# Block forms with their signs turned: one GpSimd sum becomes an accumulating DMA, the other moves to VectorE

## The chip, the cores and the metric

The kernel runs on one core of a Trainium2 chip. The metric is the device time of one execution in microseconds (us); the times of several executions are given as their median with the lowest and the highest. Five engines with queues of their own do the work: TensorE (PE in the profile, its weight loads PEld), VectorE (DVE), ScalarE (ACT), GpSimd (POOL) and SyncE (SP, which here only issues DMAs). An engine carries out its instructions in the order in which they stand in its queue, and an instruction that has to wait holds everything behind it.

## The reference

One layer of an encoder over 512 tokens of width 1024, in float32. What matters here are the projections: products of a weight matrix with the normed activations.

```python
def hybrid_mixer(h, w_in, ...):
    p = h @ w_in
    q, k, v, z, cb, cc, cx, gates = jnp.split(p, SPLIT_IDX, axis=-1)
    ...                                     # three branches ya, yb, yc of width 512
    br_d = jnp.einsum("bsnc,ncd->bsnd", br, w_branch)
    g = jax.nn.sigmoid(gates.reshape(bsz, seq, N_BRANCHES, D_MODEL))
    return jnp.sum(g * br_d, axis=2) @ w_out

def memory_cross_attention(h, mem, mem_g, wq, wk, wv, wo):
    m = rms_norm(mem, mem_g)
    q = (h @ wq).reshape(bsz, seq, XA_HEADS, XA_HEAD_DIM)
    ...

def swiglu(h, w_gate, w_up, w_down):
    return (jax.nn.silu(h @ w_gate) * (h @ w_up)) @ w_down
```

The layer is x + mixer(norm x), then + attention into 256 memory tokens, then + swiglu, and a last norm.

## The kernel before

**Two halves for each factor.** A float32 factor goes to TensorE as a rounded part "hi" (float32r, made by a cast on ScalarE) and the remainder "lo" = value - hi (a subtraction on VectorE). A product is three passes: hi x hi, hi x lo, lo x hi. In tile names a last h or l tells the two (wh, wl; hTh, hTl; h3h, h3l). A weight block arrives in a raw tile wr (three buffers), loaded by SyncE as soon as a buffer is free.

**Seven products for eight.** The gates of the mixer (class Branch, 11 steps of 256 columns), the queries of the cross-attention (Query, 4 steps) and the gate and up projections of the feed-forward (Gate and Up in turn, 20 steps) use the class Seven. It cuts the weight block and the activations in 2 x 2 blocks (rows 0-511 and 512-1023 of the inner dimension; 128 columns; 256 tokens) and makes the 2 x 2 block product from 7 block products, with sums and differences of blocks, the forms: s1 to s4 on the weight side, t1 to t4 on the activation side. Inside the raw tile `r[:, 0:4, 0:P]` and `r[:, 0:4, P:256]` are the two upper blocks, `r[:, 4:8, ...]` the lower ones. The form s1 has a tile s of its own; s3 is put in place of the upper right block, s2 in place of the upper left one and s4 in place of the lower left one.

**Steps.** `seven_open` prepares the first item, and `seven_run` goes through the items with one step each. In step k TensorE multiplies item k (n in the code) and finishes two products of the one before (p), while the other engines make the forms, casts and remainders of the one after (q). A step has these products in this order on TensorE: l11 with r11 and s1 with t1 of item n, s4 with r22 of item p, s2 with t2 of n, l22 with t4 of p, l12 with r21 of n (into a bank pfb), s3 with t3 of n; 12 matmuls of 256 columns each. Branch steps end with 24 matmuls of 512 columns (pbr), from a fourth kind of weight tile, wb.

**Who makes what before the change.** For item q: GpSimd makes s1 (L251) and then s3 (L252); VectorE makes s2 from them (L257) and s4 (L258); ScalarE casts the left blocks, s1 and the pair (s2, s4) in one instruction (L268), and VectorE takes the remainders (L273). The blocks s3 and l22 are the right half of the raw tile; they are cast only in the next step, at its beginning, in one instruction of 1024 elements a partition (`n.hi(("s3", "l22"), n.right)`). Only for the first item of the feed-forward stage does VectorE make s1 and s3 too. In the results, ScalarE copies a product out of PSUM (L287, tiles m and u) and VectorE adds the next one to it (L886, L1362 and others, called c11, c22, c12 in the code).

**What sets the order.** All of this in Seven is pinned: it stands on its engine in the order of the code. The rest is ordered by a list scheduler when the program is built.

## Time and profile before

| | us |
|---|---|
| median of 3 runs (lowest to highest) | 945.65 (945.56 to 946.8) |
| the profiled execution | 946.39 |
| its span, first to last instruction | 944.4 |
| PE busy / PEld busy in it | 933.3 / 846.9 |
| DVE busy | 717.8 |
| ACT busy | 500.3 |
| POOL busy | 241.0 |

Busy time counts an engine's instructions; what the engine waited for stands in the view of waits. The profiled execution is 0.74 us above the median and within the range of the runs; 1.99 us of it lie outside its span. A row of the timeline has the start, the duration (of the first to the last, where several are merged), engine, line, operation, tiles with sizes, how many, and in brackets the idle time before it and what ended it. The stages that use Seven are Branch (about 241 to 404 us), Query (501 to 545) and Gate/Up (637 to 831).

### The profile page before, as it was taken

How to read it: one execution, taken by the hardware profiler on the slowest of the kernel's cores; microseconds unless marked ns; L12 is line 12 of the kernel's file. 1: busy time of each engine (PE TensorE's matmuls, PEld its weight loads, DVE VectorE, ACT ScalarE, POOL GpSimd, SP SyncE). 2: the span in 40 equal slices, each digit the busy share in tenths (PEclk: the TensorE clock that was granted, in tenths of full speed). 3: DMA queues.
4: the chain of work that ended last, by engine and by line, in shares of the span. 5: the costliest groups of instructions: out<-in, count | busy, mean ns of one | idle time of the engine just before them, and what ended most of it. 6: DMA issues, size and time to landing. Idle time of an engine off the chain costs nothing.

```text
span 944.4 us, 14872 instructions
## 1 busy us (share of the span) xinstructions
PE 933.3 (99%) x6054; PEld 846.9 (90%) x6054; DVE 717.8 (76%) x891; ACT 500.3 (53%) x780; POOL 241.0 (26%) x216
## 2 busy tenths in 40 slices
PE   8999999999999999999999999999999999999997
PEld 8988888888999999988989998899999999988885
DVE  6787887658866666576897783498888888777996
ACT  6574665334544344356754762555555545557452
POOL 0221122254311535230013000024535454201000
PEclk9999999999999999999999999999999999999999
DMA  8421221320333323272352421114233332376622
GB/s 290 157 90 51 84 79 56 123 90 23 112 107 117 110 92 112 90 266 91 142 171 90 133 91 45 45 46 134 91 115 110 101 123 92 110 268 150 243 99 89
DMA packets 84276, 109.24 MB, mean 116 GB/s; under 512 B 2176, under 2 KB 63664, under 8 KB 84208
## 3 DMA queue, kind: packets, MB, share of 16 engines
q1 hardware_dynamic: 82384, 101.74, 32.5%
q0 software_dynamic: 1824, 6.55, 2.6%
q8 instruction: 47, 0.77, 0.3%
q14 instruction: 21, 0.17, 0.1%
HBM read 104.10 MB, written 2.10 MB: 112 GB/s over the span
## 4 chain that ended last, share of the span: by engine, by line
PE 94%; DVE 2%; ACT 1%; DMA 1%; issue 1%; SPq 0%; POOL 0%; POOLq 0%; DVEq 0%; ACTq 0%
PE pf L281 29%; PE pb L143 9%; PE pn L143 7%; PE pbr L929 7%; PE pc L143 6%; PE pfb L281 5%; PE pq L143 4%; PE pb L1432 4%; PE pf L143 4%; PE pa L1432 3%; PE pc L1432 3%; PE pk L143 2%; PE pv L494 2%; PE z L694 2%; PE po L143 1%; PE sc L143 1%
## 5 line engine op out<-in xcount | busy, mean ns | idle before, releaser
L273 DVE TENSOR_TENSOR wl<-wr,wh 128x1024 fp32r<-128x1024 f32 x105 | 152.8, 1465 | 33.6 <-ACT wh L268 33.6
L268 ACT CAST wh<-wr 128x1024 fp32r<-128x1024 f32 x105 | 110.3, 1053 | 31.7 <-DVE wr L258 31.7
L106 DVE TENSOR_TENSOR wl<-wr,wh 128x1024 fp32r<-128x1024 f32 x68 | 83.6, 1244 | 33.0 <-ACT wh L105 23.4
L105 ACT CAST wh<-wr 128x1024 fp32r<-128x1024 f32 x68 | 70.2, 1051 | 41.8 <-PE pb L143 19.3
L251 POOL TENSOR_TENSOR s<-wr 128x512 f32<-128x512 f32 x34 | 45.2, 1328 | 166.3 <-DVE w L273 126.7
L287 ACT COPY u<-pf 128x256 f32<-128x256 f32 x70 | 26.2, 374 | 100.3 <-DVE g L1362 31.5
L252 POOL TENSOR_TENSOR wr<-wr 128x512 f32<-128x512 f32 x34 | 71.1, 2091 | 2.7
L177 POOL TENSOR_TENSOR rs<-ve,mhalf 128x1 f32<-128x1 f32 x18 | 10.8, 602 | 228.4 <-DVE ve L175 228.4
L937 POOL TENSOR_TENSOR merged<-merged,sg 128x512 f32<-128x512 f32 x16 | 26.8, 1679 | 80.7 <-DVE sg L936 80.7
L711 POOL TENSOR_SCALAR_AFFINE_SELECT ab<-ab 128x128 f32<-128x128 f32 x32 | 23.6, 770 | 79.8 <-ACT ab L708 79.8
L287 ACT COPY m<-pf 128x256 f32<-128x256 f32 x35 | 13.0, 373 | 46.5 <-PE pf L281 45.7
L281 PE MATMUL pf<-h3th,wh 128*128 128x256 f32 x240 | 37.0, 276 | 0.0
L281 PE MATMUL pf<-h3tl,wh 128*128 128x256 f32 x240 | 37.0, 276 | 0.0
L281 PE MATMUL pf<-h3th,wl 128*128 128x256 f32 x240 | 37.0, 276 | 0.0
L258 DVE TENSOR_TENSOR wr<-wr 128x512 f32<-128x512 f32 x35 | 33.0, 943 | 1.2
L1468 ACT CAST wh<-wr 128x1024 fp32r<-128x1024 f32 x20 | 20.8, 1053 | 21.2 <-PE pc L1432 9.6
L281 PEld LDWEIGHTS pf<-h3th,wh 128*128 128x128 f32 x240 | 31.7, 188 | 0.1
L281 PEld LDWEIGHTS pf<-h3th,wl 128*128 128x128 f32 x240 | 31.7, 188 | 0.0
L281 PEld LDWEIGHTS pf<-h3tl,wh 128*128 128x128 f32 x240 | 31.7, 188 | 0.0
L186 ACT ACTIVATE jk<-xr 128x512 f32<-128x512 f32 x24 | 15.1, 630 | 24.4 <-DVE xr L1019 13.5
L257 DVE TENSOR_TENSOR wr<-s,wr 128x512 f32<-128x512 f32 x35 | 23.9, 684 | 4.7 <-POOL wr L252 4.3
L1389 POOL TENSOR_TENSOR afb<-afb,g 128x256 f32<-128x256 f32 (+1 forms) x16 | 18.4, 1153 | 34.7 <-DVE afb L1362 34.7
(433 smaller groups left out, 2717.0 us busy)
## 6 DMA issues: line engine op xcount, KB each, us to landing
wr<-in_w_in_dram SPq DMA_DIRECT2D x26, 1024.0 KB, 5.4
wr<-in_w_down_ffn_dram SPq DMA_DIRECT2D x13, 1024.0 KB, 5.8
wr<-in_w_gate_ffn_dram SPq DMA_DIRECT2D x11, 1024.0 KB, 5.6
wr<-in_w_up_ffn_dram SPq DMA_DIRECT2D x11, 1024.0 KB, 5.3
wb<-in_w_branch_dram SPq DMA_DIRECT2D x12, 512.0 KB, 3.4
wr<-in_w_out_dram SPq DMA_DIRECT2D x4, 1024.0 KB, 8.5
wr<-in_w_k_xa_dram SPq DMA_DIRECT2D x4, 1024.0 KB, 8.3
wr<-in_w_v_xa_dram SPq DMA_DIRECT2D x4, 1024.0 KB, 5.0
```

What stands on the lines that cost most here:

```text
L105: nc.scalar.copy(out=hi, in_=src)
L106: nc.vector.tensor_tensor(out=lo, in0=src, in1=hi, op=ALU.subtract)
L143: mm = nc.tensor.matmul(dst, a(i), b(j), start=first and n == 0, stop=last and n == tot - 1)
L251: pin(self.eng.tensor_tensor(out=self.s1, in0=r[:, 0:4, P:256], in1=r[:, 4:8, P:256], op=ALU.add))
L252: pin(self.eng.tensor_tensor(out=r[:, 0:4, P:256], in0=r[:, 0:4, 0:P], in1=r[:, 0:4, P:256], op=ALU.subtract))
L258: pin(nc.vector.tensor_tensor(out=r[:, 4:8, 0:P], in0=r[:, 4:8, 0:P], in1=r[:, 0:4, 0:P], op=ALU.subtract))
L268: pin(nc.scalar.copy(out=t[0], in_=src))
L273: pin(nc.vector.tensor_tensor(out=l, in0=src, in1=h, op=ALU.subtract))
L281: pin(nc.tensor.matmul(dst[:, 0:256], w[:, k, :], v[:, k, :], start=first and n == 0, stop=last and n == 11, skip_group_check=True))
L287: pin(nc.scalar.copy(out=m, in_=self.a[:, 0:256]))
L929: pin(nc.tensor.matmul(pbr, self.wb[w][:, i, j * P:(j + 1) * P], y[v][:, i, :], start=m == 0, stop=m == 3 * CT - 1))
L1432: pin(nc.tensor.matmul(dst, a[u][:, k, :], w[v][:, k, :], start=first and n == 0, stop=last and n == 5, skip_group_check=True))
```

## The change

The forms on the activation side that were subtracted one way round are subtracted the other way, so that on the weight side every form is a sum. With R11, R12, R21, R22 for the raw weight blocks: s1 = R12 + R22 as before, s3 = R12 + R11 (was R11 - R12), s2 = s1 + R11 (was s1 - s3), s4 = R21 + s2 (was R21 - s2). s3 is now added up in place by two accumulating DMAs of 256 KB each on GpSimd's queue; s1 is made on VectorE; s2 is written into the tile of s1 and no longer needs s3. So (s2, s4) no longer lie side by side, and their cast and their remainder become two instructions of 512 elements each. Some products come out with the other sign, which is put right where they are used: by `scale=-1.0` of an activation, or by the new helper `minus` (-a - b in one VectorE instruction) or another scalar_tensor_tensor in place of a tensor_tensor.

```diff
+    def minus(o, a, b):
+        return nc.vector.scalar_tensor_tensor(out=o, in0=a, scalar=-1.0, in1=b, op0=ALU.mult, op1=ALU.subtract)
...
     class Seven:
-        eng = nc.gpsimd
...
         def sums(self):
             r = self.raw
             self.s1 = self.fp.tile([P, 4, P], F32, name=nm("s1"), tag="s1", bufs=1)
-            pin(self.eng.tensor_tensor(out=self.s1, in0=r[:, 0:4, P:256], in1=r[:, 4:8, P:256], op=ALU.add))
-            pin(self.eng.tensor_tensor(out=r[:, 0:4, P:256], in0=r[:, 0:4, 0:P], in1=r[:, 0:4, P:256], op=ALU.subtract))
+            pin(nc.vector.tensor_tensor(out=self.s1, in0=r[:, 0:4, P:256], in1=r[:, 4:8, P:256], op=ALU.add))
+            for k in (0, 2):
+                pin(nc.gpsimd.dma_start(out=r[:, k:k + 2, P:256], in_=r[:, k:k + 2, 0:P], accum_op=ALU.add))
 
         def sums2(self):
             r = self.raw
-            pin(nc.vector.tensor_tensor(out=r[:, 0:4, 0:P], in0=self.s1, in1=r[:, 0:4, 0:P], op=ALU.subtract))
-            pin(nc.vector.tensor_tensor(out=r[:, 4:8, 0:P], in0=r[:, 4:8, 0:P], in1=r[:, 0:4, 0:P], op=ALU.subtract))
+            pin(nc.vector.tensor_tensor(out=self.s1, in0=self.s1, in1=r[:, 0:4, 0:P], op=ALU.add))
+            pin(nc.vector.tensor_tensor(out=r[:, 4:8, 0:P], in0=r[:, 4:8, 0:P], in1=self.s1, op=ALU.add))
...
-            pin(nc.scalar.copy(out=t[0], in_=src))
-            return t, src
+            n = t[0].shape[1] // len(src)
+            got = [(t[0][:, i * n:(i + 1) * n], t[1][:, i * n:(i + 1) * n], v) for i, v in enumerate(src)]
+            for h, l, v in got:
+                pin(nc.scalar.copy(out=h, in_=v))
+            return got
...
     # prepare and seven_run
             if q:
-                q.sums2()
+                q.lo(c)
...
             if q:
-                q.lo(c)
+                q.sums2()
...
-                b = q.hi(("s2", "s4"), q.left)
+                b = q.hi(("s2", "s4"), q.s1, q.left[:, 4:8])
...
     # right_forms, query_forms and forms_right, the activation side, three places like this one
-        for o, a, b in ((r11, r12, r11), (r12, r22, r12), (r22, r22, r11), (r21, r21, r22)):
+        for o, a, b in ((r11, r11, r12), (r12, r22, r12)):
             nc.vector.tensor_tensor(out=o, in0=a, in1=b, op=ALU.subtract)
+        minus(r22, r22, r11)
+        minus(r21, r22, r21)
...
     # where the results are used
         def gate22(self):
-            self.silu(self.g[:, 1, HT[1]], self.g[:, 1, HT[1]])
+            self.silu(self.g[:, 1, HT[1]], self.g[:, 1, HT[1]], -1.0)
...
     class Up(Gate):
         def c22(self, p, m):
-            self.add(self.af[:, 1, HT[1]], p, m)
+            pin(minus(self.af[:, 1, HT[1]], p, m))
...
         def c21(self, p):
-            self.mul_g(nc.vector, 1, HT[0], p)
+            pin(nc.vector.scalar_tensor_tensor(out=self.af[:, 1, HT[0]], in0=p, scalar=-1.0,
+                                               in1=self.gate.g[:, 1, HT[0]], op0=ALU.mult, op1=ALU.mult))
...
-    items[0].eng = nc.vector
```

On GpSimd the sums go and two DMA issues stand in their place. The rows are those of two steps of the Gate/Up stage, an Up item's products af in the middle; wr is a raw weight tile, s the tile of s1. Before:

```order
L251 TENSOR_TENSOR s_7218<-wr_7079 128x512
L252 TENSOR_TENSOR wr_7079<-wr_7079 128x4x128
L251 TENSOR_TENSOR s_7340<-wr_7202 128x512
L252 TENSOR_TENSOR wr_7202<-wr_7202 128x4x128
L1389 TENSOR_TENSOR afb<-afb,g_7185 128x256
L1389 TENSOR_TENSOR afb<-afb,g_7185 128x512
L251 TENSOR_TENSOR s_7463<-wr_7324 128x512
L252 TENSOR_TENSOR wr_7324<-wr_7324 128x4x128
```

And after the change:

```order
L254 DMA wr_7145<-wr_7145 128x2x128 x2
L254 DMA wr_7271<-wr_7271 128x2x128 x2
L1402 TENSOR_TENSOR afb<-afb,g_7254 128x256
L1402 TENSOR_TENSOR afb<-afb,g_7254 128x512
L254 DMA wr_7396<-wr_7396 128x2x128 x2
L254 DMA wr_7522<-wr_7522 128x2x128 x2
```

The two DMAs of an item stand where its two sums stood, ahead of the products of the same step.

On VectorE one step of the same stage, from the sum c11 of one item to that of the next; wl and w are remainders, g the tile of the sums. Before:

```order
L1362 TENSOR_TENSOR g_7185<-pfb_7171,m_7101 128x256
L1362 TENSOR_TENSOR g_7185<-pf_7082,u_7199 128x256
L273 TENSOR_TENSOR wl_7222<-wr_6957,wh_7221 128x1024
L273 TENSOR_TENSOR wl_7253<-wr_7079,wh_7252 128x1024
L1362 TENSOR_TENSOR g_7185<-pf_7082,u_7151 128x256
L257 TENSOR_TENSOR wr_7079<-s_7218,wr_7079 128x4x128
L258 TENSOR_TENSOR wr_7079<-wr_7079 128x4x128
L273 TENSOR_TENSOR w_7257<-s_7218,w_7256 128x512
L273 TENSOR_TENSOR wl_7291<-wr_7079,wh_7290 128x1024
```

After:

```order
L1375 TENSOR_TENSOR g_7254<-pfb_7239,m_7168 128x256
L1375 TENSOR_TENSOR g_7254<-pf_7148,u_7268 128x256
L252 TENSOR_TENSOR s_7287<-wr_7145 128x512
L278 TENSOR_TENSOR wl_7292<-wr_7020,wh_7291 128x1024
L278 TENSOR_TENSOR wl_7323<-wr_7145,wh_7322 128x1024
L1375 TENSOR_TENSOR g_7254<-pf_7148,u_7217 128x256
L278 TENSOR_TENSOR w_7327<-s_7287,w_7326 128x512
L259 TENSOR_TENSOR s_7287<-s_7287,wr_7145 128x512
L260 TENSOR_TENSOR wr_7145<-wr_7145,s_7287 128x4x128
L278 TENSOR_TENSOR wl_7361<-s_7287,wh_7360 128x512
L278 TENSOR_TENSOR wl_7361<-wr_7145,wh_7360 128x512
```

The sum s1 (L252) has come in behind the two sums of the results, the remainder of s1 now stands ahead of the sums s2 and s4, and the last remainder is in two halves.

On ScalarE the entry of the Branch stage: the casts of the first item (left blocks; s1; s2 and s4; then s3 with l22, wr again), and the first copy out of PSUM, m. Before:

```order
L268 CAST wh_2151<-wr_2144 128x1024
L268 CAST w_2157<-s_2146 128x512
L268 CAST wh_2161<-wr_2144 128x1024
L268 CAST wh_2212<-wr_2144 128x1024
L287 COPY m_2215<-pf_2195 128x256
```

After:

```order
L273 CAST wh_2152<-wr_2144 128x1024
L273 CAST w_2156<-s_2146 128x512
L273 CAST wh_2162<-s_2146 128x512
L273 CAST wh_2162<-wr_2144 128x512
L273 CAST wh_2216<-wr_2144 128x1024
L292 COPY m_2219<-pf_2198 128x256
```

Only the cast of (s2, s4) is cut in two; the cast of s3 with l22, the second from below, is where it was, and now it reads what the two DMAs have written.

TensorE's 6,054 matmuls stand in the same order in both programs, with the same operands at the same addresses in SBUF and PSUM, and so do SyncE's DMAs.

## The prediction

> **What bounds the kernel now.** I read the page's busy times first, then what TensorE waited for, then the chain that ended last, and last the busy time in the three stages that the change touches.

> ```profile
> span 944.4 us, 14872 instructions
> ...
> PE 933.3 (99%) x6054; PEld 846.9 (90%) x6054; DVE 717.8 (76%) x891; ACT 500.3 (53%) x780; POOL 241.0 (26%) x216
> ```

> TensorE is busy for 933.3 of 944.4 us. So at most 11.1 us could be won without taking matmuls away, and the change takes none away. Where the idle time lies is the next question: the view of waits, TensorE alone, all of its rows.

> ```profile
> PE warm L527 <- POOL ident masks.py:199: 1.4, 1, 1.4
> PE pc L143 <- DVE kk L657: 0.9, 1, 0.9
> PE pv L494 <- ACT hTh L469: 0.8, 1, 0.8
> PE pv L494 <- ACT wvh L478: 0.7, 1, 0.7
> ```

> Four waits with a releaser, 3.8 us in all, at lines of the first norm and of the attention branch (tiles warm, pv, kk); no line of Seven is among them. A busy TensorE is not yet one at its best pace, since the ends of matmuls are modelled. The chain that ended last has the pace in its rows: of a Branch step (the first) and of a Gate/Up step (the two others).

> ```profile
> 246.85 8.34 PE pf L281 x72
> ...
> 642.14 8.16 PE pf L281 x72
> 650.30 1.36 PE pfb L281 x12
> ```

> A Gate/Up step is 84 matmuls in 9.52 us, 113.3 ns each, and the chain goes through TensorE alone. The stages by windows (Branch, Query, Gate/Up):

> ```profile
> 245.43:400.63 155.20, 155.20 (x1106) 145.47 (x1106) 102.45 (x126) 67.99 (x114) 51.15 (x31) 1.00 0.34 109
> 501.67:542.00 40.33, 40.25 (x347) 40.06 (x346) 33.69 (x54) 26.50 (x50) 7.02 (x4) 1.00 0.37 122
> 636.68:824.40 187.72, 187.72 (x1646) 186.87 (x1646) 158.13 (x187) 100.18 (x168) 84.38 (x55) 1.00 0.35 110
> ```

> The columns are the length, then busy time of PE, PEld, DVE, ACT and POOL with instructions, granted clock, DMA share, GB/s. In all three the matmul unit is idle for 0.08 us together, at a granted clock of 1.00. This is the ceiling of what a quicker VectorE or GpSimd can win there. The order of the matmuls and their addresses stay, so only two things can move the time: a wait that the new order brings, or another pace.

> **The sums leave GpSimd.** These are the two sums of a step on GpSimd, and VectorE's remainders:

> ```profile
> L273 DVE TENSOR_TENSOR wl<-wr,wh 128x1024 fp32r<-128x1024 f32 x105 | 152.8, 1465 | 33.6 <-ACT wh L268 33.6
> ...
> L251 POOL TENSOR_TENSOR s<-wr 128x512 f32<-128x512 f32 x34 | 45.2, 1328 | 166.3 <-DVE w L273 126.7
> ...
> L252 POOL TENSOR_TENSOR wr<-wr 128x512 f32<-128x512 f32 x34 | 71.1, 2091 | 2.7
> ```

> 116.3 us of GpSimd go, off the path. What they did to others stands in a Gate/Up step of the timeline, all engines:

> ```profile
> 680.32 1.29 POOL L251 TENSOR_TENSOR s<-wr 128x512 f32<-128x512 f32 x1 [1.23 <-DVE w L273]
> ...
> 680.76 1.93 DVE L273 TENSOR_TENSOR wl<-wr,wh 128x1024 fp32r<-128x1024 f32 x1 [0.19 <-ACT wh L268]
> ...
> 681.69 2.15 POOL L252 TENSOR_TENSOR wr<-wr 128x512 f32<-128x512 f32 x1
> ...
> 683.14 0.37 ACT L287 COPY u<-pf 128x256 f32<-128x256 f32 x1 [2.41 <-DVE g L1362]
> ...
> 683.54 0.43 DVE L1362 TENSOR_TENSOR g<-pf,u 128x256 f32<-128x256 f32 x1 [0.52 <-ACT u L287]
> ...
> 684.14 0.62 PE L281 MATMUL pf<-h3h,wh 128*128 128x256 f32 x4
> ...
> 684.49 1.22 DVE L273 TENSOR_TENSOR wl<-wr,wh 128x1024 fp32r<-128x1024 f32 x1 [0.53 <-ACT wh L268]
> ...
> 685.75 0.37 SPq L114 DMA_DIRECT2D wr<-in_w_gate_ffn_dram  x1
> ...
> 685.88 0.63 ACT L268 CAST w<-s 128x512 fp32r<-128x512 f32 x1
> ...
> 687.68 0.37 ACT L287 COPY u<-pf 128x256 f32<-128x256 f32 x1 [1.17 <-DVE g L1362]
> ...
> 692.68 1.05 ACT L268 CAST wh<-wr 128x1024 fp32r<-128x1024 f32 x1
> ```

> The same remainder takes 1.93 us beside GpSimd's sums and 1.22 us without, 0.71 more. That one counts: behind it on VectorE stands c11, then ScalarE copies u, then VectorE's c22 (683.54 to 683.97) reads the bank to which TensorE adds from 684.14 on. The margin is 0.17 us. It grows to about 0.9 us, which wins nothing today, since TensorE does not wait there.

> **s1 on VectorE, and the halves.** VectorE makes the same sum once before, in the entry of the feed-forward stage, and a scalar_tensor_tensor of 512 elements stands beside it:

> ```profile
> 629.60 0.69 DVE L251 TENSOR_TENSOR s<-wr 128x512 f32<-128x512 f32 x1
> ```

> ```profile
> 224.87 0.75 DVE L844 SCALAR_TENSOR_TENSOR un<-pg,chan,un 128x512 f32<-128x512 f32 x1
> ```

> Per step VectorE gains 0.69 us for s1 and 2 x 0.69 - 1.22 = 0.16 us for the halved remainder; `minus` instead of a tensor_tensor costs at most 0.75 - 0.69 = 0.06 us, at most twice in a step. Against this stand the 0.71 us that it no longer loses: +0.3 us in a Gate/Up step. Its idle time there is (187.72 - 158.13) / 20 = 1.5 us a step, which hides it. The new sum stands behind c22, so it does not delay TensorE's margin of above; behind it wait the remainders of s3 and l22 (before at 684.49, after an idle 0.53 us), so they start some 0.2 us later, while s3 is multiplied only at the end of the step. ScalarE gains 2 x 0.63 - 1.05 = 0.2 us a step and idles (187.72 - 100.18) / 20 = 4.4 us: hidden. The remainder of s1, moved ahead of s2 and s4, fills the time in which ScalarE casts them. The form changes on the activation side swap one instruction for one: nothing. Scales inside activations: nothing, the instructions were there. SyncE's queue is the same, and a raw buffer comes free at the same remainder as before.

> **The accumulating DMAs.** Two issues of 256 KB stand on GpSimd's queue per step. Before, the kernel has four such DMAs of 512 KB in the last stage (line 1471):

> ```profile
> L1471 POOL DMA_DIRECT2D wl<-wx x4: 847/871/921, 855.7 to 867.3; - x4
> ...
> DMA to landing us min/median/max: 4.5/5.5/6.2
> ```

> GpSimd is held 0.87 us by an issue, so 70 of them give back 61 of the 116 us. VectorE's instructions beside them were not slowed (the sums of the same stage, min/median/max in ns):

> ```profile
> L1476 DVE TENSOR_TENSOR wx<-wr,wx x3: 1217/1221/1227, 856.5 to 863.4; 128x1024 f32<-128x1024 f32 x3
> ```

> From the first issue to the second landing I reckon 0.9 us plus the landing of one DMA. The low end is 0.9 + 4.5 = 5.4 us. For the high end I take the longest landing of any big DMA on GpSimd's queue, the loads of x:

> ```profile
> L1064 POOL DMA_DIRECT2D xr<-in_x_dram x4: 528/551/588, 402.8 to 404.4; - x4
> ...
> DMA to landing us min/median/max: 3.9/5.7/7.8
> ```

> 0.9 + 7.8 = 8.7 us. I take 0.9 + 5.5 = 6.4 us, by the accumulating row, which moves as many bytes as the pair; what the rows don't show is pieces of 512 bytes where those have 4 KB. [...]

> Is 6.4 us early enough? In Gate/Up the new s1 ends at 683.97 + 0.69 = 684.7, the pair lands at 691.1, and the cast of s3 and l22 begins at 692.68: 1.6 us to spare. The cast holds ScalarE's queue, but in the step behind it ScalarE idles 1.17 us before the copy u; TensorE would feel the pair only beyond 684.7 + L = 692.68 + 1.17, that is L over 9.2 us. The entry of Branch is tighter, since the cast follows in the same step (timeline, rows of three engines):

> ```profile
> 235.63 1.21 DVE L918 TENSOR_TENSOR wl<-wb,wh 128x1024 fp32r<-128x1024 f32 x1
> ...
> 240.42 2.00 ACT L268 CAST wh<-wr 128x1024 fp32r<-128x1024 f32 x2 [2.29 <-DVE wr L258]
> ...
> 242.72 0.37 ACT L287 COPY m<-pf 128x256 f32<-128x256 f32 x1 [0.30 <-PE pf L281]
> ...
> 245.46 0.37 ACT L287 COPY u<-pf 128x256 f32<-128x256 f32 x1 [0.89 <-PE pf L281]
> ...
> 246.68 0.64 PE L281 MATMUL pf<-hTth,wh 128*128 128x256 f32 x4
> ```

> s1 stands behind the remainder at 235.63, ends at 237.5, and the pair lands at 243.9. The second of the two casts began at 241.4: 2.5 us late, and the copies m and u wait behind it. ScalarE's idle times (0.30 and 0.89) and the time from u's end at 245.83 to the matmul that overwrites its bank at 246.68 (0.85) take up 2.04. So 0.46 us would reach TensorE; without GpSimd's sums VectorE gets to s1 up to 0.7 us sooner. I take half, 0.2 us, once. In the feed-forward's entry s1 ends at 630.3, and in Query the cast likewise comes a step later: nothing.

> **The sum.** 0.08 us at most to win, 0.2 us to pay: the profiled 946.39 stays what it is, and so does the median, 945.65, which is 0.74 us lower; 945.8.

> **Rivals.** *Slower: the pair lands late.* With L = 8.7 us the Branch entry loses 237.5 + 8.7 - 241.4 - 2.04 = 2.8 us: 948.5. It decides from about L = 8 us, where this term passes 1.9 us and is seen. Above 9.2 us each of 20 Gate/Up steps would pay the excess too; at 10.2 us up to 20 us: 966. For it: pieces of 512 bytes are untried in this trace, and a weight load of 1 MB is issued in the same part of each step (685.75). Against it: the four accumulating DMAs, issued from 855.7 to 867.3, landed in at most 6.2 us, and from 857.7 on such loads were issued beside them (SyncE's queue, timeline):

> ```profile
> 857.70 17.01 SPq L1493 DMA_DIRECT2D wr<-in_w_down_ffn_dram  x4
> ```

> [...] Chances: 0.15 for the entry, of which 0.03 by that rule, and 0.06 for the steps.

> *Faster: GpSimd's reading slows matmuls.* Branch takes 8.34 us for 72 where Gate/Up takes 8.16, 2.5 ns a matmul. If GpSimd's sums did that, 11 Branch and 4 Query steps of 84 would win 15 x 84 x 2.5 ns = 3.2 us: 942.5. Against it: Gate/Up has the same sums on GpSimd (680.32) and keeps 113.3 ns. Chance 0.07.

> *Nothing is seen*, with the terms as summed: 0.72. Its own range is 945.3 (rounding of the runs below the median) to 947.2 (0.2% or 1.9 us is about what a measurement of this kernel tells from no change).

> **The numbers.** Likeliest 945.8. The range reaches from 944.0, short of the faster case, to 949.5, over the Branch entry at L = 8.7 with a us to spare; the faster case and the late steps lie outside, 0.13. Faster by over 0.2%: 0.07; within: 0.72; slower: 0.21.

> **What the profile after would show.** PE's waits without a line of Seven and 9.52 us a Gate/Up step; L273's 1024-element rows near 1.22 us; DVE busy within some us of 717.8; POOL near 186; the DMA rows of line 254 landing in 5 to 7 us; ScalarE's cast of s3 waiting for a DMA at the Branch entry alone. Wrong would be casts that wait for DMAs in every step, or a TensorE that waits for VectorE's s1, remainders or c22.

## The result, and the profile after

The changed kernel takes 974.45 us (median of 4 runs, 973.14 to 975.43) against 946.22 us (4 runs, 945.56 to 950.19) for the kernel before on the same chip: 1.0288 of its time, 95% interval 1.0257 to 1.032. The prediction was 945.8, with 949.5 as the upper end of its range. The profiled execution took 974.35 us. From the page after, its first lines and the costliest group (part 5):

```profile
span 972.7 us, 15101 instructions
...
PE 942.3 (97%) x6054; PEld 851.7 (88%) x6054; DVE 728.7 (75%) x959; ACT 507.3 (52%) x815; POOL 203.8 (21%) x218
...
L254 POOL DMA_DIRECT2D wr<-wr x70 | 84.9, 1213 | 292.3 <-issue 147.2
```

GpSimd did lose work (241.0 to 203.8 us), but before the new DMAs it stood idle for 147.2 us that end in nothing the profile shows. The view of waits for TensorE alone has three lines of Seven, where before there was none (us in all, times, longest):

```profile
PE pf L286 <- ACT m L292: 12.1, 10, 3.2
PE pf L286 <- DVE g L1375: 7.3, 9, 0.8
...
PE pf L286 <- DVE afb L1420: 0.6, 3, 0.2
```

Where the time went can be had from the order of the matmuls, which is the same in both: the time from one matmul to a later one, after minus before, in the two profiled executions. It is 1.6 us more from the Branch entry through Branch, 3.4 in Query, 23.5 in Gate/Up, and 0.3 less in all the rest: 28.2 of the 28.3 us between the spans. In Gate/Up the matmuls ahead of which TensorE waits are of three kinds: 10.0 us at the start of s2·t2, which adds to the bank that ScalarE's copy m reads; 8.5 at s4·r22, which adds to the bank that VectorE's sum c22 reads; and 2.8 at s1·t1, which starts a bank that VectorE has just read. The last 2.2 us are spread over all others.

A Gate/Up pair of steps in the timeline shows both kinds of wait. First the late pair (rows of VectorE, GpSimd, ScalarE and TensorE):

```profile
715.08 0.68 DVE L252 TENSOR_TENSOR s<-wr 128x512 f32<-128x512 f32 x1
...
716.18 1.20 POOL L254 DMA_DIRECT2D wr<-wr  x1 [4.38 <-DVE s L252]
...
722.38 1.22 POOL L254 DMA_DIRECT2D wr<-wr  x1 [5.00 <-issue]
...
725.61 1.05 ACT L273 CAST wh<-wr 128x1024 fp32r<-128x1024 f32 x1 [2.59 <-DMA wr<-wr]
...
726.56 0.37 ACT L292 COPY m<-pf 128x256 f32<-128x256 f32 x1
...
726.98 0.74 PE L286 MATMUL pf<-h3th,wh 128*128 128x256 f32 x4 [0.59 <-ACT m L292]
```

s1 ends at 715.76. The second DMA of the pair has no wait in the program, yet it is issued 6.2 us after the first. The pair is there at 725.61: 9.85 us after s1, where the prediction took 6.4. ScalarE's cast of s3 waits 2.59 us, the copy m stands behind it and is late, and TensorE waits 0.59 us before s2·t2. Then the other kind, some microseconds earlier:

```profile
708.57 1.21 POOL L254 DMA_DIRECT2D wr<-wr  x1 [2.99 <-PE pf L286]
...
709.33 2.48 POOL L1402 TENSOR_TENSOR afb<-afb,g 128x256 f32<-128x256 f32 x2
709.36 3.00 DVE L260 TENSOR_TENSOR wr<-wr,s 128x512 f32<-128x512 f32 x1
...
714.74 0.42 DVE L1375 TENSOR_TENSOR g<-pf,u 128x256 f32<-128x256 f32 x1 [0.52 <-ACT u L292]
...
715.22 0.74 PE L286 MATMUL pf<-h3h,wh 128*128 128x256 f32 x4 [0.79 <-DVE g L1375]
```

Both products of Up stood on GpSimd's queue behind the second DMA of a pair. When it is issued they run one after the other, at the time when VectorE makes s4: s4 takes 3.00 us instead of 0.69, everything behind it on VectorE is late, c22 too, and TensorE waits 0.79 us before s4·r22.

### The profile page after: what moved, and what is told of

It reads as the page before. It is cut to its first block, busy times and chain, and to the rows that moved or that the text cites. A ratio compares the mean times of both kernels' runs of the same rounds, so it can differ in the third digit from the quotient of the medians.

```text
span 972.7 us, 15101 instructions
## 1 busy us (share of the span) xinstructions
PE 942.3 (97%) x6054; PEld 851.7 (88%) x6054; DVE 728.7 (75%) x959; ACT 507.3 (52%) x815; POOL 203.8 (21%) x218
## 3 DMA queue, kind: packets, MB, share of 16 engines
q0 software_dynamic: 20864, 15.73, 10.6%
## 4 chain that ended last, share of the span: by engine, by line
PE 66%; DVE 14%; issue 9%; DMA 5%; ACT 3%; POOL 3%; SPq 0%; POOLq 0%; DVEq 0%; ACTq 0%
PE pf L286 12%; PE pb L143 9%; PE pc L143 6%; PE pbr L936 6%; PE pn L143 4%; DMA wr<-wr 4%; PE pq L143 4%; PE pb L1445 4%; DVE wl L278 3%; PE pa L1445 3%; PE pc L1445 3%; PE pk L143 2%; DVE s L259 2%; PE pfb L286 2%; PE pv L499 2%
## 5 line engine op out<-in xcount | busy, mean ns | idle before, releaser
L254 POOL DMA_DIRECT2D wr<-wr x70 | 84.9, 1213 | 292.3 <-issue 147.2
L278 DVE TENSOR_TENSOR wl<-wr,wh 128x1024 fp32r<-128x1024 f32 (+1 forms) x105 | 114.6, 1097 | 41.3 <-ACT wh L273 40.9
L273 ACT CAST wh<-wr 128x1024 fp32r<-128x1024 f32 (+1 forms) x105 | 95.2, 907 | 60.6 <-DMA wr<-wr 51.5
L106 DVE TENSOR_TENSOR wl<-wr,wh 128x1024 fp32r<-128x1024 f32 x68 | 83.6, 1244 | 33.4 <-ACT wh L105 23.9
L105 ACT CAST wh<-wr 128x1024 fp32r<-128x1024 f32 x68 | 70.3, 1051 | 42.1 <-PE pb L143 19.7
L273 ACT CAST wh<-s 128x512 fp32r<-128x512 f32 x35 | 21.8, 622 | 35.5 <-DVE s L259 35.4
L259 DVE TENSOR_TENSOR s<-s,wr 128x512 f32<-128x512 f32 x35 | 38.9, 1112 | 1.2
L286 PE MATMUL pf<-h3h,wh 128*128 128x256 f32 x160 | 25.9, 284 | 7.3 <-DVE g L1375 7.3
L1481 ACT CAST wh<-wr 128x1024 fp32r<-128x1024 f32 x20 | 20.7, 1052 | 20.8 <-PE pc L1445 9.0
L260 DVE TENSOR_TENSOR wr<-wr,s 128x512 f32<-128x512 f32 x35 | 30.5, 871 | 1.2
L286 PEld LDWEIGHTS pf<-h3h,wh 128*128 128x128 f32 x160 | 21.4, 188 | 9.2 <-DVE g L1375 9.1
```

What stands on the lines that cost most here:

```text
L105: nc.scalar.copy(out=hi, in_=src)
L106: nc.vector.tensor_tensor(out=lo, in0=src, in1=hi, op=ALU.subtract)
L254: pin(nc.gpsimd.dma_start(out=r[:, k:k + 2, P:256], in_=r[:, k:k + 2, 0:P], accum_op=ALU.add))
L259: pin(nc.vector.tensor_tensor(out=self.s1, in0=self.s1, in1=r[:, 0:4, 0:P], op=ALU.add))
L260: pin(nc.vector.tensor_tensor(out=r[:, 4:8, 0:P], in0=r[:, 4:8, 0:P], in1=self.s1, op=ALU.add))
L273: pin(nc.scalar.copy(out=h, in_=v))
```

## The experiments

Three theories. R: the setting `dynamic_dma_scratch_size`, 1024 bytes in the kernel, is a reserve that GpSimd's DMAs fill (with descriptors, as the expectations call it) and that does not hold both DMAs of a pair, so the second waits for the first, and GpSimd's queue with it. P: pieces of 512 bytes are slow in themselves. V: VectorE's new work and order are too much.

**A larger reserve.** (label ring1280)

> Only the reserve for GpSimd's DMA descriptors grows, from 1024 to 1280 bytes of a partition. Theory R (the second accumulating DMA of a pair cannot be issued while the first one's descriptors fill the reserve, so the pair lands some 9.6 us after s1 and GpSimd's queue stands still): the second issue follows the first at once, 1.2 us later, GpSimd's idle time before L254 that ends in nothing shown falls from 147 us to under 40, and the time comes back from 974 to 945-952. Rival P (pieces of 512 bytes are slow in themselves, or beside the weight loads): the second issue may come earlier, but the pair still lands late and the time stays above 965. Rival V (s1, the halved remainders and the new order on VectorE are the cause): no change, 970-976.

954.0 us (5 runs; 1.0075 of the time before, interval 1.005 to 1.0101; the figures in the brackets below are the same): 20.5 of the 28.2 us come back, 2 us fewer than R expected. The view of line 254, after and then with 1280 bytes:

```profile
L254 POOL DMA_DIRECT2D wr<-wr x70: 1184/1212/1279, 236.9 to 839.2; - x70
...
  issue: 147.2, 43
...
DMA to landing us min/median/max: 3.1/3.7/7.0
```

```profile
L254 POOL DMA_DIRECT2D wr<-wr x70: 1191/1264/1778, 237.1 to 816.7; - x70
...
  issue: 43.1, 8
...
DMA to landing us min/median/max: 3.1/6.6/8.9
```

Waits that end in nothing shown fall from 43 to 8 (147.2 to 43.1 us, where R expected under 40), and most pairs are issued as one row of two (below). The trace of the changed kernel says what the 43 waits were: by its landing times, each ends 0.32 to 0.34 us after the DMA before it on the queue has landed, so a DMA was held until the one before was done. The second DMA of a pair is issued 3.5 to 7.3 us after the first in all 35 pairs of the changed kernel, and 0.7 to 1.5 us after it in all 35 with 1280 bytes. With 1280 bytes each DMA lands later, 6.6 us in the median, now that its twin is under way beside it:

```profile
243.47 0.68 DVE L252 TENSOR_TENSOR s<-wr 128x512 f32<-128x512 f32 x1
...
244.59 2.45 POOL L254 DMA_DIRECT2D wr<-wr  x2 [4.95 <-DVE s L252]
...
252.44 1.04 ACT L273 CAST wh<-wr 128x1024 fp32r<-128x1024 f32 x1 [3.04 <-DMA wr<-wr]
```

From s1's end (244.15) to the cast are 8.3 us in this Branch step, without any wait between the two issues. So R carries most. P, or another cause of a slow landing, has a part: 8.3 is near the prediction's upper bound of 8.7. V alone is out.

**How much room?** (label ring1088) The same edit with 1088 in place of 1280.

> [...]

One run, 959.16 us; 951 to 957 was expected if the second DMA follows at once, 968 to 976 if it still waits. The pairs are issued together, the second DMA 0.7 to 0.8 us behind the first in all 35. Waits that end in nothing shown are 32.7 us (5 times), none of them inside a pair; the median landing is 6.5 us. So for two DMAs of 272 packets each (GpSimd's DMA queue has 20,864 packets in the changed kernel and 1,824 before, 272 more for each of the 70) 1024 bytes are too few and 1088 are enough. How much of the reserve one DMA takes, no run shows; that 1088 would do was the author's estimate. The time is 2 us above the expected 957. Against 1280 bytes it has 2.8 us more in Query, where TensorE waits 2.2 us and the granted clock is 0.96, and 1.3 us more in Gate/Up, nearly all of which ran at TensorE's slower pace (below).

**One DMA in place of the pair.** (label one_dma) With 1280 bytes:

```diff
-            for k in (0, 2):
-                pin(nc.gpsimd.dma_start(out=r[:, k:k + 2, P:256], in_=r[:, k:k + 2, 0:P], accum_op=ALU.add))
+            pin(nc.gpsimd.dma_start(out=r[:, 0:4, P:256], in_=r[:, 0:4, 0:P], accum_op=ALU.add))
```

> As the kernel with a reserve of 1280 bytes, but one accumulating DMA of 256 KB (512 pieces of 512 bytes) in place of the pair. If the two issues of 1.2 us on GpSimd's queue make the landing late, one issue lands sooner: the cast's waits for it fall from 18 us to under 8, and the stalls of TensorE at the entries (3.3 us) go. If the pieces and the way from issue to first packet do, nothing changes: the issue takes twice as long, the landing comes 8 us behind s1, 951-958.

One run, 956.27 us. One issue of 512 pieces holds GpSimd 1.29 us (median), not twice 1.21. It saves nothing: the landing is 6.5 us in the median (9.5 at most), ScalarE's casts wait 20.2 us for it (18.4 with the pair), and TensorE waits 4.7 us for the copies m. That is the second expectation: what is slow comes after the issuing. Whether it is the pieces of 512 bytes or the weight loads beside them, no run tells apart.

**No DMA at all.** In place of the pair, one addition on GpSimd (label s3_gpsimd):

```diff
-            for k in (0, 2):
-                pin(nc.gpsimd.dma_start(..., accum_op=ALU.add))
+            pin(nc.gpsimd.tensor_tensor(out=r[:, 0:4, P:256], in0=r[:, 0:4, P:256], in1=r[:, 0:4, 0:P], op=ALU.add))
```

> The pair of accumulating DMAs is replaced by one GpSimd addition of the same 512 elements; s1 stays on VectorE, signs and order stay as after the change. Theory R and rival P both expect 945-949, since there is no DMA any more; TensorE busy 99%. Rival V expects over 960, since VectorE's work is as after the change.

951.36 us (10 runs; 1.0051, 1.0038 to 1.0063): between the two expectations, so both missed. What it loses in Gate/Up is TensorE's pace (below).

The same, and s1 on GpSimd too (label both_gpsimd):

> Both sums on GpSimd as before the change; only signs, halved remainders and the order of VectorE's instructions are as after it. R and P: 945-948. V: 946 if s1 was what VectorE could not take, above 955 if the order and the halves are.

947.75 us (10 runs; 1.0024, 1.0004 to 1.0045). By the stage times 1.8 us of it lie between Query and Gate/Up, where before VectorE made the first item's sums; Gate/Up takes 0.9 us less than before. Signs, halves and order cost nothing there.

The same addition on VectorE (`nc.vector` in the added line; label s3_vector):

> The pair of DMAs is replaced by one VectorE addition (0.69 us) right behind s1: VectorE makes all four sums, GpSimd none. R and P: VectorE gains 0.69 us a step of the 1.2 us of idle time that the prediction left it in Gate/Up, so 945-950. V: slower than the changed kernel, 975 or more.

944.08 us (10 runs; 0.9974, 0.9961 to 0.9986): 0.3% faster than the kernel before, and 0.9 us under the range that R and P expected. V is out: VectorE takes all four sums. By stages (matmul to matmul, against before) it wins 0.2 us in Query and 1.4 in Gate/Up; another 0.7 lie ahead of Branch, where the profiled executions of all versions differ by up to 1.1 us.

**VectorE in the old order.** (label before_vector) The kernel before with `eng = nc.vector` for every Seven.

> The kernel before with one word changed: all sums of Seven on VectorE, signs, order and whole remainders as before. If what made the version with all four sums on VectorE 0.26% faster than before is only that GpSimd no longer reads beside VectorE, this one gains as much: 943.5-945. If the new order and the halved remainders are needed for it, VectorE's 1.4 us more per step reach TensorE here: 947 or more.

945.74 us (12 runs; 0.9996, 0.9988 to 1.0004): no change, between the two expectations, so both missed. The two versions were timed against before on different chips, but their intervals do not overlap. So the changed signs, with the order and the halved remainders that go with them, are worth some 1.7 us once VectorE makes every sum. In the profiled executions Gate/Up differs by 1.9 us; the pace below says why.

**The queue behind the DMA.** (label products_vector) The changed kernel, 1024 bytes, with Up's products on VectorE:

```diff
-            pin(nc.gpsimd.tensor_tensor(out=o, in0=o, in1=self.gate.g[:, j, cs], op=ALU.mult))
+            pin(nc.vector.tensor_tensor(out=o, in0=o, in1=self.gate.g[:, j, cs], op=ALU.mult))
```

> The changed kernel with Up's products on VectorE instead of GpSimd; the pairs of DMAs stay as they are. Theory R has two ways from the held-up issue to TensorE: the pair lands late (the stalls before s3 t3, which end in ScalarE's copy m, about 10 us of the page's 12) and the products queue on GpSimd behind the held-up DMA and then run beside VectorE's sums, which makes c22 late (the stalls before s4 r22 and l22 t4, about 10 us). With the products gone from that queue the second kind should go and the first stay: 962-967. Rival V (VectorE simply has too much work): more work on VectorE, so slower than the changed kernel: 976-990.

963.22 us (4 runs; 1.0185, 1.0163 to 1.0206), as R expected. (The waits that this expectation puts before s3 t3 and l22 t4 are those before s2·t2 and s1·t1.) TensorE's waits for VectorE at lines of Seven are gone from the view of waits, those for the copy m stay:

```profile
PE pf L286 <- ACT m L292: 11.2, 7, 3.2
PE warm L532 <- POOL ident masks.py:199: 1.4, 1, 1.4
PE pc L143 <- DVE kk L662: 0.9, 1, 0.9
```

VectorE has 20 instructions more and the kernel is 11 us quicker; VectorE's busy time even falls, from 728.7 to 717.2 us, since its sums are no longer slowed. So the 11 us came from the products that were held up on GpSimd's queue and then ran beside VectorE's sums, not from VectorE's load. In the profiled executions Gate/Up gives back 12.7 us; Query, where nothing was changed, takes 2.4 us more at a granted clock of 0.92.

**The entries.** (label gateup_vector) The pairs in Branch and Query alone; `pin(nc.vector.tensor_tensor(...))` for s3 in Gate/Up.

> The changed kernel with the pairs of DMAs in Branch and Query alone; in Gate/Up s3 is added on VectorE. The traces put 1.6 us of the change's loss at the Branch entry and 3.4 at the Query entry. If these are all that the pairs cost outside Gate/Up, the time is that of the version with all sums on VectorE and 5 us: 948-950. If the late pairs cost more than the two stalls shown, over 951.

951.44 us (10 runs; 1.0047, 1.0033 to 1.0062), so the second expectation: 1.4 us above the range of the first. Gate/Up is as good as with all sums on VectorE (1.4 us less than before), Branch costs 1.6 us more than before and Query 4.8, not 3.4. In Query's window the granted clock (the last column but two) is 0.96, where it was 1.00 in the changed kernel's:

```profile
500.00:545.00 45.00, 41.85 (x331) 41.03 (x330) 31.45 (x52) 24.13 (x46) 7.24 (x6) 0.96 0.43 102
```

**What remains: TensorE's pace.** With 1280 bytes the kernel is still 8.1 us slower than before on the same chip. The view of waits has 3.1 us of it for TensorE at Seven's lines (3 waits, each before s2·t2 in the second step of a stage), and the version with s3 on GpSimd has hardly any stall and yet is 5.5 us slower. The chain that ended last has it, a row for 12 and one for 72 matmuls. Version with s3 on GpSimd:

```profile
690.75 1.41 PE pfb L286 x12
692.16 8.48 PE pf L286 x72
```

With 1280 bytes, where the pace changes:

```profile
674.23 8.16 PE pf L286 x72
682.39 1.36 PE pfb L286 x12
683.75 8.56 PE pf L286 x72
692.31 1.41 PE pfb L286 x12
693.72 8.48 PE pf L286 x72
```

And the kernel before, rows of the same chain that the prediction did not look at:

```profile
697.90 1.36 PE pfb L281 x12
699.26 8.41 PE pf L281 x72
...
709.03 8.16 PE pf L281 x72
...
718.55 8.39 PE pf L281 x72
```

8.16 us is 113.3 ns a matmul, 8.48 is 117.8, at a granted clock of 1.00 in both. Nothing is in between: by the starts of the matmuls, both versions run at 113.3 up to a short stall before s4·r22 (0.14 us with 1280 bytes, 0.23 with s3 on GpSimd) and at 117.8 from there to the end of Gate/Up, some 1,240 matmuls, 5.5 us. The kernel before has a stall of 0.10 to 0.12 us in every second step from 703 us on, six in all, and goes on at 113.3 each time. Since the next matmul comes 0.11 us late too, each costs 0.23 us (the rows of 8.41 and 8.39). With all sums on VectorE in the new order there is none: that is the 1.4 us which this version wins in Gate/Up. In the old order on VectorE there is one of 0.10 us, at 779 us, and 117.8 ns from then on. The changed kernel has both paces too: behind its first long wait in Gate/Up, 0.99 us at 670 us, it runs at 117.8 ns up to the next.

To see whether a stall sets the pace, ten delays of c22 were put into the version with all sums on VectorE (label stall_map):

```diff
+            for c in self.again if name == "u3" else ():
+                pin(nc.scalar.copy(out=m[:, 0:c], in_=self.a[:, 0:c]))
             pin(nc.scalar.copy(out=m, in_=self.a[:, 0:256]))
```

> The version with all four sums on VectorE; in Gate steps alone ScalarE makes its copy u3 some columns longer (the same columns again, 672 to 1064 more), so that c22 ends later by a different amount in each and TensorE stalls shortly before s4 r22 in most. Theory M (a short stall sets the pace: TensorE goes on with 113.3 or with 117.8 ns a matmul until the next stall): behind some of the ten stalls the two following steps run at 117.8 ns, behind others at 113.3, with no DMA of GpSimd in the stage. Rival (117.8 ns come from the accumulating DMAs or from GpSimd's sums): all steps at 113.3 between the stalls.

One run, 955.56 us. In the first Gate step TensorE does not stall, in the second it stalls for 0.53 us; from it on TensorE runs at 117.8 ns for two steps, until the third, of 0.15 us, sets it back to 113.3; after the other seven (1.1 to 1.5 us) it stays at 113.3. Three windows of 18 us, ahead of the second stall, behind it and behind the third (matmuls in the bracket behind PE's busy time, the granted clock last but two):

```profile
645.00:663.00 18.00, 18.00 (x162) 18.00 (x161) 17.07 (x24) 9.66 (x19) 2.72 (x2) 1.00 0.37 117
666.00:684.00 18.00, 18.00 (x155) 18.00 (x154) 16.10 (x23) 9.58 (x19) 2.66 (x2) 1.00 0.38 118
686.00:704.00 18.00, 18.00 (x162) 18.00 (x161) 16.14 (x23) 9.59 (x19) 2.66 (x2) 1.00 0.37 117
```

162 matmuls, 155 and 162 in the same time, with no DMA of GpSimd in the stage: theory M holds for this kernel. Which stall leads to which pace doesn't go by its length (0.10, 0.14, 0.23, 0.53 and 0.99 us led to 117.8; 0.10, 0.12, 0.15, 0.56 and 1.1 to 113.3); that stays open.

Last, GpSimd's sums without their worst place (label s3_alternate): as the version with s3 on GpSimd, but in Gate/Up every second s3 on VectorE.

```diff
+    for u in items[1::2]:
+        u.eng = nc.vector
```

> As the version with s3 added on GpSimd (951.4 us), but in the Gate/Up stage every second s3, the one made during a Gate step, is added on VectorE, so that no sum of GpSimd makes VectorE late where c22 had the least time to spare. Theory M (one stall of 0.23 us at 686 us left TensorE at 117.8 ns a matmul for the rest of the stage): without it the stage runs at 113.3 throughout and the time falls by 1250 x 4.5 ns = 5.6 us, to 945-947. Rival (117.8 ns come from the GpSimd sums themselves, half of which are still there): 948-951, with steps at 117.8.

949.49 us (10 runs; 1.0027, 1.0014 to 1.004), so the median missed the 945 to 947 that theory M expected and lies in the rival's range, though it came 1.9 us under the version it changes. The profiled execution is the fastest of the ten, 947.43 us; in it the whole of Gate/Up runs at 113.3 ns, its stalls are 0.05 to 0.08 us (one of 0.22 at its end), and the stage takes 4.5 us less than with s3 on GpSimd. Half of GpSimd's sums are still there, and the profiled execution with both sums on GpSimd (label both_gpsimd) runs Gate/Up at 113.3 ns too; so these sums alone don't make the slower pace. The other nine have no trace, so whether they switched is not shown.

## Why the prediction was wrong

- **TensorE bounds it; only a wait or another pace can move the time:** right, and both did.
- **The pair of DMAs, the step that failed.** "From the first issue to the second landing I reckon 0.9 us plus the landing of one DMA" took for granted that the second issue follows the first. It came 6.2 us later in the step shown, 0.32 us after the first had landed; the four DMAs of line 1471, some 4 us apart, could not tell. With 1088 bytes of reserve it comes 0.7 to 0.8 us after the first. With 1024, L, reckoned from s1's end as the prediction did, came to 9.85 us in Gate/Up and to 11.2 in Query; the bound of 8.7 was made of rows that don't have this wait.
- **The terms of that sum** were small as well: an issue took 1.21 us, not 0.87 (70 of them 84.9 us, not 61), and a landing beside its twin 6.6 us, not 5.5. Without the wait between the two, the 6.4 would still have been 8.3 us, as in the Branch step shown. An error of fact stands in the prediction and in the section on the change: the two DMAs have 128 KB each, not 256 (the pair has 256), so the row of line 1471 moved twice the pair's bytes, in 128 pieces of 4 KB, and still landed sooner than the pair's 512 pieces.
- **What is queued behind the waiting instruction** was not named: Up's products on GpSimd. Taking them away brought 11 us. This is the largest thing that the working left out.
- **What waits behind the late cast.** The prediction held that s3 is multiplied only at the end of the step. But its cast stands on ScalarE's queue ahead of the copy m, and s2·t2, in the middle of the step, adds to the bank that m copies. That is where TensorE waited.
- **The thresholds.** Gate/Up, "L over 9.2 us": the figure fits, the path doesn't. L of 9.85 gave a wait of 0.59 us where 0.65 follows, but the wait came by the copy m in the same step, not by the copy u in the step behind. By m the rows of before give 684.7 + L = 692.68 + 1.01, so L over 9.0; that the two are close is luck. The two rows of before behind the cast at 692.68:

```profile
693.64 0.37 ACT L287 COPY m<-pf 128x256 f32<-128x256 f32 x1
...
695.02 0.62 PE L281 MATMUL pf<-h3th,wh 128*128 128x256 f32 x4
```

- **The Branch entry:** wrong. I followed the copy u (2.04 us of cover); TensorE met the copy m first, whose cover in the trace of before is 0.30 us ahead of it and 0.81 behind (243.09 to the matmul at 243.90). The pair was there at 243.85, as reckoned (243.9), but by luck: s1 ended 1.1 us sooner and L was 7.5 us, not 6.4. So the cast came 2.45 us late; less 1.11 that is 1.34, and 1.44 was measured, not 0.2. The rows are one of before and two of after:

```profile
243.90 0.62 PE L281 MATMUL pf<-hTth,wh 128*128 128x256 f32 x4
```

```profile
243.85 1.04 ACT L273 CAST wh<-wr 128x1024 fp32r<-128x1024 f32 x1 [2.56 <-DMA wr<-wr]
...
245.22 0.74 PE L286 MATMUL pf<-hTth,wh 128*128 128x256 f32 x4 [1.44 <-ACT m L292]
```

- **The Query entry:** "nothing" was never worked out; the wait was 3.16 us, in the trace after:

```profile
504.22 0.68 DVE L252 TENSOR_TENSOR s<-wr 128x512 f32<-128x512 f32 x1
...
505.59 1.19 POOL L254 DMA_DIRECT2D wr<-wr  x1 [7.72 <-DVE s L252]
...
512.82 1.22 POOL L254 DMA_DIRECT2D wr<-wr  x1 [6.04 <-issue]
...
516.07 1.04 ACT L273 CAST wh<-wr 128x1024 fp32r<-128x1024 f32 x1 [4.53 <-DMA wr<-wr]
...
517.43 0.74 PE L286 MATMUL pf<-h2th,wh 128*128 128x256 f32 x4 [3.16 <-ACT m L292]
```

- **VectorE:** right. s1 and the halves fit into its idle time; with all four sums on it the kernel is the fastest. That TensorE does not wait for c22 in the kernel before was wrong: I quoted a step of the chain in which it doesn't, and from 703 us on it loses 0.23 us in every second step. So the 0.08 us "at most to win" was wrong as well; 1.4 us could be won in Gate/Up. The windows count TensorE as busy there.
- **The rival that came true** is the one for the steps (966, given a chance of 0.06), mainly by another cause than those given for it: not slow pieces, but a held issue. In the chances, the 0.03 of the entry's 0.15 for an issue slowed by a working VectorE was the author's estimate, and no run shows it: of the 70 issues, 1184 to 1279 ns each, 11 lay wholly beside VectorE's instructions (1184 to 1252 ns) and one beside none (1217 ns).
- **The rival on matmul pace** had the wrong cause: with no sum on GpSimd, Branch (after its entry) takes as long as before (8.34 us for 72 matmuls in both).

## What to carry to other kernels

Before two DMAs go on GpSimd's queue one behind the other, try whether the room reserved for them (`dynamic_dma_scratch_size`) holds both: here 1024 bytes did not hold two of 272 packets each, and 1088 did. With 1024 the second waited without a row of its own until the one before had landed (it was issued 0.32 to 0.34 us after that), and everything behind it on GpSimd waited too. A page on which GpSimd is idle before a DMA "until issue" for 147 us can mean just this; what it ends with, the landing of the DMA before, tells. And read every row of the chain in a stage that repeats, not one: 0.23 us in every second step was there to be seen.

## What the runs showed of the hardware

In Gate/Up TensorE ran the same stream of 256-column matmuls and weight loads at one of two paces, 113.3 and 117.8 ns, at the same granted clock. It switched at stalls of 0.1 to 1.0 us, though not at all of them, and then stayed for up to 1,240 matmuls. So a stall of 0.14 us was followed by a loss of 5.5 us. With 1024 bytes of reserve a GpSimd DMA was issued 0.32 to 0.34 us after the landing of the one before (43 times in 70); with 1088 the second of each pair came 0.7 to 0.8 us after the first. An accumulating DMA of 512 pieces of 512 bytes holds GpSimd for 1.29 us, one of 256 pieces for 1.21. Behind the stall of 2.2 to 3.2 us in Query the granted clock of that window fell to 0.96, 0.96 and 0.92 in three of the experiments, not in the changed kernel, where the stall was 3.2 us too.
